# Half of a weight loaded beside the attention, the prompt's operand sums spread over the steps, and a load count in the last product

## The chip, the cores and the metric

The kernel runs on one NeuronCore of one Trainium2 chip. The metric is the device time of one execution in microseconds. The engines have names of their own in the profile: PE (TensorE, the matrix multiplier), PEld (its weight loads), DVE (VectorE), ACT (ScalarE), POOL (GpSimd) and SP (SyncE, which issues nearly all DMA transfers of this kernel). A name with a q behind it (SPq) is the engine's queue.

## The reference, cut to what matters

One layer of an encoder is run for two batches with the same weights: a prompt of 512 tokens and a sample of 1024 tokens, both 1024 channels wide, all in float32.

```
h = rmsnorm(x, norm_attn_g)
z = h @ w_in                                   # q, k, v, ca, cb
a = window_attention(q, k, v, bias, sink)      # 8 heads, 2 key/value heads, |q-k| <= 128
c = ca * sigmoid(cb)
c = dwconv31(c) + b
c = silu(layernorm(c))
x = x + concat(a, c) @ w_out
h = rmsnorm(x, norm_ffn_g)
u = dwconv3(h @ w_up) + b                      # 2 * 2816 channels
x = x + (silu(u[:2816]) * u[2816:]) @ w_down
y = rmsnorm(x, norm_final_g)
```

## The kernel before, in words

**Products.** Every float32 operand of a product is cut into a high and a low part (`hi` is a cast on ACT, `lo` a subtraction on DVE or POOL), and three matmuls stand for one: hi·hi, hi·lo, lo·hi. A matmul takes a 128x128 weight tile and 512 columns. Tokens are worked in blocks of 128: blocks 0 to 3 are the prompt, 4 to 11 the sample.

**Stages.** First comes the projection with w_in (lines 503 to 590 and 871 to 880) with the prompt's attention beside it. Then the prompt's product with w_out (`prompt_out`, line 848). Then the prompt's feed-forward up-projection: 22 steps of `ffn_step` (line 973), each of two halves of 24 matmuls; beside it runs the sample's attention, which is a generator that is advanced a piece at a time. After it come the sample's product with w_out, block by block (`out_blocks`, line 1156; each block has two halves of 512 columns, 24 matmuls a half), the sample's up-projection in a fast form with seven products a step (`first` to `seventh`, loop at line 1611, 22 steps j), and last the down-projection of both batches, again with seven products of 11 steps each (`down_step`, line 1573; the seventh product stands in a loop of its own from line 1666, with the final normalisation between its steps).

**What runs beside.** The queue `side` holds generators. `tick` (line 267) is called some times in each product and advances `side` by `pace["rate"]` pieces a call; `drain(side)` runs it to its end. `sample` (line 990) is the generator that matters here. It yields the sample's attention; then waits until the feed-forward is at its step 21 (`KW`); then loads w_out (16 pieces of 256 KB, `load_wo`, line 789) and cuts each into hi and lo (`split_wo`, line 799), first and second half of the columns in turn, five pieces behind the loads; then runs `conv_norm` (line 713: four transposes, layer norm, four transposes, the swish and the cut into hi and lo) for blocks 4 and 5. Those blocks' product needs for its first four chunks (kc 0 to 3) the attention's result, fetched back from DRAM by `load_cat` (line 708), and for its last four (kc 4 to 7) what `conv_norm` leaves. Behind the feed-forward stands `drain(side)` at line 1018, and only then the sample's blocks in order: both halves of block 4, both of block 5, and so on (line 1162).

**Sums of the prompt.** The down-projection's fast form needs sums and differences of pairs of the prompt's gated columns. `sums_of` (line 961) fetches a pair by two DMAs, makes four results on POOL (lines 966 to 969, 128x256 each) and stores them by two DMAs. In the loop over j it is called whole, at every second step from j = 2, and once more at j = 18; 11 pairs in all.

**Loads of the down-projection.** `ahead` is the list of its 185 loads in order of need; `load_next(n)` issues the next n of them, if there are any left (line 1391). `down_step` asks for three a step while fewer than 24 are held; the last loop asks for two (line 1667); `operands` asks for what is still missing.

**What sets the order.** Storage in SBUF is cut into slots (`Slots`, line 65): 15 of 4096 bytes a partition (`q`), 4 of 4352 (`c`), 61 of 2048 (`h`), 2 of 2304 (`d`). A tile takes the smallest free slot that it fits, the one that has been free longest first, and waits for whatever last read that slot. A planner (`schedule_with_timeline_sim=True`) orders the instructions of each engine by a simulated timeline, from the order in which the program issues them and what each waits for. Within `by_hand` (from line 1304) PE's order is the order written, and in the down-projection SP's too; DVE, ACT and POOL are ordered by the planner throughout.

Of the kernel before, what the change touches and what calls it, by code (L numbers as in the profile page):

```python
# [50 lines left out]
SCB, SCD = "aapa", "aaap"  # L51


WOP, WOA, DW, DW2 = 1, 5, 2, 2
NE = 2
YN = 2
OB = "cbu"
NW = 16
BL = 9
SA = 4  # L60
AP = 1
KW = 21


class Slots:
# [35 lines left out]
def tile_hybrid_encoder(ctx: ExitStack, tc: tile.TileContext, xs, rel_bias, norm_attn_g, w_in,  # L101
# [687 lines left out]
    def load_wo(kc, n):  # L789
        raw = wor[kc, n] = sb.tile([NT])  # L790
        nc.sync.dma_start(raw[:], laid["w_out"][n, :, kc, :])
# [98 lines left out]
    while out:  # L890
        if side:
            for _ in range(AP):
                if side:
                    advance(side)
            if not side:
                pace.update(late=CLO)
        advance(out)
        n += 1
        if n > 7:
            next(doubling, None)  # L900
        if n % SA == 0 and n > 18:
            next(units_of_sample)
    drain(convs)

# [56 lines left out]
    def sums_of(p):  # L961
        e, t, x, y = (sb.tile([2, HT]) for _ in range(4))
        nc.sync.dma_start(e[:], gap[1, 8][:, p])
        nc.sync.dma_start(t[:], gap[2, 4][:, p])
        eng = nc.gpsimd
        eng.tensor_tensor(x[:, 1, :], e[:, 1, :], t[:, 1, :], op=ALU.add)
        eng.tensor_tensor(x[:, 0, :], e[:, 0, :], e[:, 1, :], op=ALU.subtract)
        eng.tensor_tensor(y[:, 0, :], x[:, 1, :], e[:, 0, :], op=ALU.subtract)
        eng.tensor_tensor(y[:, 1, :], t[:, 0, :], y[:, 0, :], op=ALU.subtract)
        nc.sync.dma_start(gap[7, 5][:, p], x[:])  # L970
        nc.sync.dma_start(gap[6, 3][:, p], y[:])

    def ffn_step(k):
# [13 lines left out]
    want_up_raw(1, 0)  # L987
    at = [0]

    def sample():  # L990
        yield from units_of_sample
        while at[0] < KW:
            yield 0.0
        kt.clear(), vt.clear(), qt.clear(), bias.clear()
        use.update(norm="a")
        pace.update(rate=RN)
        for m in range(16 + WOA):
            if m in (10, 12):
                load_cat(m // 2 - 1)
            if m < 16:  # L1000
                load_wo(m // 2, m % 2)
            if m >= WOA:
                split_wo((m - WOA) // 2, m % 2, m % 4 < DW2)
                yield 0.0
        drain(late)
        for m in range(NE):
            yield from conv_norm(4 + m)

    pace.update(rate=RD, late=CD)
    for k in range(NJ):  # L1010
# [4 lines left out]
    h2.clear()  # L1015
    use.update(out=OB, turn="u")
    pace.update(rate=RE)
    drain(side)

# [137 lines left out]
        if n == 1:  # L1159
            scaled(i)  # L1160

    for i in range(4, NB - 2):
        if i + NE < NB:
            side.appendleft(conv_norm(i + NE))
        if i == 8:
            side.append(turned(1, old_bank))
        for n in range(2):
            out_blocks(i, n)
    reserve(4)
    for j in range(2):  # L1170
        for half in range(2):
# [401 lines left out]
    def down_step(k):  # L1573
# [33 lines left out]
        if i == 4 and p == 8:  # L1607
            with_x("o12", 0, 1)
            load_x1(1, 0)

    for j in range(2, NJ):
        for half in range(2):
            load_up(j + 3, half)
        if j >= NJ - 3:
            sb.free.extend(raws.free)
            raws.free.clear()
        if j >= NJ - 2:
            load_next(4)
        split_up(j + 1, 1, 2)
        if (j - 2) // 2 < NPAIR and j % 2 == 0:  # L1620
            sums_of((j - 2) // 2)
        if j == NJ - 4:
            sums_of(NPAIR - 1)
        second(j)
        sums_up(j + 1)
        sixth(j)
        split_up(j + 1, 5)
        last = j == NJ - 1
        value_part(j - 1)
        if last:  # L1630
            fourth(j, None, True)
            third(j)
        first(j + 1)
        split_up(j + 1, 6)
        seventh(j, None, not last)
        if last:
            by_hand.__exit__(None, None, None)
            by_hand = tc.manual_schedule(engines={mybir.EngineType.SP, mybir.EngineType.PE})
            by_hand.__enter__()
            load_next(10)  # L1640
            down_step(0)
        fifth(j + 1)
        split_up(j + 1, 7)
        if last:
            y_sum(j)
        else:
            fourth(j)
        gate_part(j)
        split_up(j + 1, 4)
        if not last:  # L1650
            third(j)
        split_up(j + 1, 3)
# [11 lines left out]
    z = wide()  # L1664
    OTHER = {1: 2, 3: 3, 4: 8, 6: 9, 8: 10, 9: 11}
    for p in range(NPAIR):
        load_next(2)
        make(base + p + 4)
        for tt in (0, 1):
            mm_down(z[:, tt * NT:(tt + 1) * NT], 3, p, tt)  # L1670
        if p == HOLD:
            zp = wide()
        if p >= HOLD:
            for q in range(p + 1) if p == HOLD else (p,):
                for tt in (4, 5):
                    mm_down(zp[:, (tt - 4) * NT:(tt - 3) * NT], 3, q, tt)
                hp.pop((3, q))
        if p == 4:
            for tt in (2, 3):
                zs.append(wide())  # L1680
                armed(zs[-1][:, L], hl[3, p][0][0])
                nc.scalar.copy(zs[-1][:, L], cut(o12, tt))
        if p in OTHER:
            blk = OTHER[p]
            tt = blk + 2 if blk < 4 else blk - 8
            finish(blk, (cut(u, tt), cut(e, tt)), False)
# [81 lines left out]
```

## Time and profile before

| | |
|---|---|
| median of 3 runs | 1514.33 us (1513.03, 1514.33, 1521.08) |
| the profiled execution | 1514.8 us, of which the span from its first to its last instruction is 1513.0 us |
| PE busy | 1480.5 us (98% of the span) |
| DVE, ACT, POOL busy | 1106.2, 801.7, 785.1 us |
| mean granted clock of TensorE | 0.992 |
| moved by DMA | 228.19 MB, 151 GB/s over the span |

The profile is of one execution. Busy time is the union of an engine's instructions; matmuls are pipelined and their ends are modelled, so that one of 0.39 us starts some 0.23 us after the one before it. "PEclk" is the clock that was granted to TensorE, 1.00 being full. A line such as "PE b L771 <- POOL h L803: 2.2, 1, 2.2" in the table of waits says: PE, before an instruction of line 771 that writes a tile named b, waited for an instruction of line 803 on POOL that writes a tile named h; 2.2 us in total, once, 2.2 us the longest. Line 1032 is the helper `sub`, 1029 the helper `add`, 1036 the helper `split_of`, 154 and 155 the helper `split`, 143 `load_x`, 148 `chunk_raw`.

### The profile page before, as it was taken

What the parts mean: (1) busy time and instruction counts of PE and PEld (TensorE: products, weight loads), DVE (VectorE), ACT (ScalarE), POOL (GpSimd) and SP (SyncE); (2) the same over time, 40 slices, a digit from 0 to 9 for tenths busy, and PEclk for the clock granted to TensorE, in tenths of its full rate; (3) what the DMA queues carried; (4) which work ended last, traced back from release to release, by engine and by line L of the source; (5) the groups of instructions that cost most, each with busy time, mean ns of one, the idle gap of its engine ahead of it and who ended that gap; (6) DMA issues with size and microseconds to landing.
All of it is one profiled execution on the core that took longest, in us unless ns stands there. A gap on an engine that the chain in (4) does not pass through costs nothing. (4 is left out here: it accounts for less than half of the span.)

```text
span 1513.0 us, 19880 instructions
## 1 busy us (share of the span) xinstructions
PE 1480.5 (98%) x6736; PEld 1216.5 (80%) x6736; DVE 1106.2 (73%) x1508; ACT 801.7 (53%) x1421; POOL 785.1 (52%) x691
## 2 busy tenths in 40 slices
PE   8999999999999999999999999999999999999997
PEld 7888788877888888778788788888888888888876
DVE  7877945648999895665767888888776855657865
ACT  6424455467777876653464445444454453443345
POOL 3454353356987875342436566565565211215666
PEclk9999999999999999999999999999999999999998
DMA  9455241843443444763124333333343473446744
GB/s 372 168 162 150 85 108 36 252 145 126 147 129 129 132 139 136 260 203 99 70 73 151 132 133 126 127 126 130 129 151 123 164 272 102 133 151 213 236 155 162
DMA packets 125201, 228.19 MB, mean 151 GB/s; under 512 B 20483, under 2 KB 45827, under 8 KB 124972
## 3 DMA queue, kind: packets, MB, share of 16 engines
q1 hardware_dynamic: 123564, 225.32, 45.4%
q10 hardware_dynamic: 1536, 1.61, 0.3%
q8 instruction: 53, 0.87, 0.2%
q14 instruction: 48, 0.39, 0.1%
HBM read 166.83 MB, written 61.10 MB: 151 GB/s over the span
## 5 line engine op out<-in xcount | busy, mean ns | idle before, releaser
L155 POOL TENSOR_TENSOR q<-q,q 128x1024 fp32r<-128x1024 f32 x66 | 158.6, 2406 | 76.2 <-ACT q L154 58.4
L1032 DVE TENSOR_TENSOR h<-h,h 128x512 fp32r<-128x512 f32 (+1 forms) x155 | 134.3, 891 | 82.9 <-ACT h L1036 36.4
L1032 POOL TENSOR_TENSOR q<-q,q 128x512 fp32r<-128x512 f32 x81 | 117.1, 1455 | 116.4 <-ACT q L1134 116.4
L1477 PE MATMUL w<-h,h 128*128 128x512 f32 x444 | 173.7, 391 | 1.3 <-ACT h L1460 0.8
L1479 PE MATMUL w<-h,h 128*128 128x512 f32 x436 | 170.1, 390 | 0.0
L1478 PE MATMUL w<-h,h 128*128 128x512 f32 x428 | 167.4, 391 | 2.8 <-DVE h L1032 2.8
L289 PE MATMUL u<-h,q 128*128 128x512 f32 x384 | 151.2, 395 | 0.3 <-DVE h L251 0.3
L291 PE MATMUL u<-h,q 128*128 128x512 f32 x384 | 150.4, 392 | 0.0
L290 PE MATMUL u<-h,q 128*128 128x512 f32 x384 | 150.2, 392 | 0.0
L1148 PE MATMUL w<-h,q 128*128 128x512 f32 x368 | 143.9, 391 | 2.9 <-ACT w L1237 2.6
L1150 PE MATMUL w<-h,q 128*128 128x512 f32 x368 | 143.7, 391 | 0.0
L1149 PE MATMUL w<-h,q 128*128 128x512 f32 x347 | 135.5, 390 | 0.0
L1032 POOL TENSOR_TENSOR h<-h,h 128x512 fp32r<-128x512 f32 (+1 forms) x36 | 48.5, 1348 | 161.9 <-ACT h L1460 109.6
L1036 ACT CAST h<-h 128x512 fp32r<-128x512 f32 x119 | 71.4, 620 | 109.3 <-DVE h L1032 43.6
L1477 PEld LDWEIGHTS w<-h,h 128*128 128x128 f32 x444 | 83.8, 189 | 19.7 <-ACT h L1460 1.2
L154 ACT CAST q<-q 128x1024 fp32r<-128x1024 f32 x66 | 69.1, 1049 | 54.5 <-PE u L290 31.1
L326 DVE SCALAR_TENSOR_TENSOR c<-d,cvw,c 128x512 f32<-128x512 f32 x128 | 95.9, 749 | 1.6
L1478 PEld LDWEIGHTS w<-h,h 128*128 128x128 f32 x428 | 80.7, 189 | 20.0 <-DVE h L1032 3.4
L1479 PEld LDWEIGHTS w<-h,h 128*128 128x128 f32 x436 | 82.1, 188 | 17.1
L1032 POOL TENSOR_TENSOR c<-q,c 128x512 fp32r<-128x512 f32 x46 | 72.5, 1586 | 41.8 <-ACT c L1134 41.8
L318 POOL TENSOR_TENSOR h<-h,h 128x512 f32<-128x512 f32 x62 | 80.5, 1300 | 17.9 <-ACT h L317 15.7
L1148 PEld LDWEIGHTS w<-h,q 128*128 128x128 f32 x368 | 69.1, 188 | 18.6 <-ACT w L1237 3.0
(455 smaller groups left out, 4010.9 us busy)
## 6 DMA issues: line engine op xcount, KB each, us to landing
q<-in_laid_w_up SPq DMA_DIRECT2D x88, 512.0 KB, 3.8
ga<-q SPq DMA_DIRECT2D x65, 256.0 KB, 2.2
h<-gap SPq DMA_DIRECT2D x57, 256.0 KB, 3.5
h<-ga SPq DMA_DIRECT2D x57, 256.0 KB, 3.2
h<-in_w_down SPq DMA_DIRECT2D x52, 256.0 KB, 3.3
q<-in_laid_w_in SPq DMA_DIRECT2D x22, 512.0 KB, 3.9
gap<-h SPq DMA_DIRECT2D x44, 256.0 KB, 2.8
q<-in_x_sample SPq DMA_DIRECT2D x15, 512.0 KB, 7.1
```

What stands on the lines that cost most here:

```text
L155: (nc.vector if dve else nc.gpsimd).tensor_tensor(lo[:], raw[:], hi[:].bitcast(F32), op=ALU.subtract)
L289: nc.tensor.matmul(out, whi[:, kc, :], hi[:], start=(kc == 0), stop=False)
L290: nc.tensor.matmul(out, whi[:, kc, :], lo[:], start=False, stop=False)
L291: nc.tensor.matmul(out, wlo[:, kc, :], hi[:], start=False, stop=(kc == KC - 1))
L326: nc.vector.scalar_tensor_tensor(acc[:], src(t), w(t), acc[:], op0=ALU.mult, op1=ALU.add)
L1032: (eng or nc.vector).tensor_tensor(out, a, b, op=ALU.subtract)
L1148: nc.tensor.matmul(out, whi[:, s], hi[:], start=(start and c == 0), stop=False, **go)
L1149: nc.tensor.matmul(out, whi[:, s], lo[:], start=False, stop=False, **go)
L1150: nc.tensor.matmul(out, wlo[:, s], hi[:], start=False, stop=(stop and c == 3), **go)
L1477: nc.tensor.matmul(out, sh[:, c], th[:], start=(p == 0 and not seeded), stop=False, **go)
L1478: nc.tensor.matmul(out, sh[:, c], tl[:], start=False, stop=False, **go)
L1479: nc.tensor.matmul(out, sl[:, c], th[:], start=False, stop=(p == NPAIR - 1), **go)
```

## The change

- `sample` no longer waits for step 21. From step 16 (`KL`) on, while the attention still runs, the first half of w_out's columns is loaded, in four pairs of 512 KB; a pair takes a slot of 4096 bytes or more.
- When the attention has ended, block 4's attention result is loaded, then the second half of w_out a piece at a time, each beside the cut of a piece of the first half; then `conv_norm(4)`; then the cuts of the second half, with block 5's load at their third; then, behind the last of them (`WN`), `conv_norm(5)`. Three of four cuts have their subtraction on DVE and one on POOL (`DW2` 3; half and half before).
- The `drain(side)` behind the feed-forward goes. The sample's blocks start with (4, first half), (5, first half), (4, second half), (5, second half), and before each the side queue is advanced until that block's `conv_norm` and the last piece of that half of w_out are there.
- `sums_of` becomes a generator with four stops, advanced three times a step of j from j = 2; what may be left is made at the start of the last step. Its first store is issued right behind the second result.
- `load_next(2)` in the last product's loop becomes `load_next(LN)` with `LN` = 3.
- In the loop over `prompt_out` a second period `SA2` is used from n = 99 on; it is 4, as `SA` is.

```diff
-WOP, WOA, DW, DW2 = 1, 5, 2, 2
+WOP, WOA, DW, DW2 = 1, 5, 2, 3
-SA = 4
+SA, N2, SA2 = 4, 99, 4
+KL, WN = 16, 7
+LN = 3
-KW = 21
...
+        yield
         eng = nc.gpsimd
         eng.tensor_tensor(x[:, 1, :], e[:, 1, :], t[:, 1, :], op=ALU.add)
+        yield
         eng.tensor_tensor(x[:, 0, :], e[:, 0, :], e[:, 1, :], op=ALU.subtract)
+        nc.sync.dma_start(gap[7, 5][:, p], x[:])
+        yield
         eng.tensor_tensor(y[:, 0, :], x[:, 1, :], e[:, 0, :], op=ALU.subtract)
+        yield
         eng.tensor_tensor(y[:, 1, :], t[:, 0, :], y[:, 0, :], op=ALU.subtract)
-        nc.sync.dma_start(gap[7, 5][:, p], x[:])
         nc.sync.dma_start(gap[6, 3][:, p], y[:])
...
+    fit = set()
+
+    def fitted(i):
+        yield from conv_norm(i)
+        fit.add(i)
+
     def sample():
-        yield from units_of_sample
-        while at[0] < KW:
+        for _ in units_of_sample:
             yield 0.0
+            if at[0] >= KL and not wor:
+                for kc in range(0, KC, 2):
+                    load_wo_pair(kc, 0)
         kt.clear(), vt.clear(), qt.clear(), bias.clear()
...
-        for m in range(16 + WOA):
-            if m in (10, 12):
-                load_cat(m // 2 - 1)
-            if m < 16:
-                load_wo(m // 2, m % 2)
-            if m >= WOA:
-                split_wo((m - WOA) // 2, m % 2, m % 4 < DW2)
-                yield 0.0
+        load_cat(4)
+        for kc in range(KC):
+            load_wo(kc, 1)
+            split_wo(kc, 0, kc % 4 < DW2)
+            yield 0.0
         drain(late)
-        for m in range(NE):
-            yield from conv_norm(4 + m)
+        yield from fitted(4)
+        for kc in range(KC):
+            if kc == 2:
+                load_cat(5)
+            split_wo(kc, 1, kc % 4 < DW2)
+            yield 0.0
+            if kc == WN:
+                yield from fitted(5)
...
-    drain(side)
...
-    for i in range(4, NB - 2):
-        if i + NE < NB:
-            side.appendleft(conv_norm(i + NE))
-        if i == 8:
+    turns_out = [(4, 0), (5, 0), (4, 1), (5, 1)] + [(i, n) for i in range(6, NB - 2) for n in range(2)]
+    for i, n in turns_out:
+        if n == 0:
+            (side.append if i < 8 else side.appendleft)(fitted(i + NE))
+        if (i, n) == (8, 0):
             side.append(turned(1, old_bank))
-        for n in range(2):
-            out_blocks(i, n)
+        while not (i in fit and (KC - 1, n) in wo):
+            advance(side)
+        out_blocks(i, n)
...
+    prompt_sums = chain(*(sums_of(p) for p in range(NPAIR)))
     for j in range(2, NJ):
...
+        if j == NJ - 1:
+            for _ in prompt_sums:
+                pass
...
-        if (j - 2) // 2 < NPAIR and j % 2 == 0:
-            sums_of((j - 2) // 2)
-        if j == NJ - 4:
-            sums_of(NPAIR - 1)
+        next(prompt_sums, None)
         second(j)
         sums_up(j + 1)
+        next(prompt_sums, None)
         sixth(j)
...
         first(j + 1)
         split_up(j + 1, 6)
+        next(prompt_sums, None)
         seventh(j, None, not last)
...
-        load_next(2)
+        load_next(LN)
```

More of the change, by code (lines that the diff above doesn't have):

```diff
@@ L900, in tile_hybrid_encoder @@
             next(doubling, None)
-        if n % SA == 0 and n > 18:
+        if n > 18 and n % (SA if n < N2 else SA2) == 0:
             next(units_of_sample)
```

## The prediction

> **What bounds the kernel now.** I read the page's busy shares first, then busy time by stage, then PE's waits, and last the instructions around the longest of those waits.
>
> ```profile
> PE 1480.5 (98%) x6736; PEld 1216.5 (80%) x6736; DVE 1106.2 (73%) x1508; ACT 801.7 (53%) x1421; POOL 785.1 (52%) x691
> ...
> 560.00:630.00 70.00, 70.00 (x340) 58.49 (x339) 42.18 (x85) 41.78 (x84) 33.86 (x29) 1.00 0.52 159
> 630.00:665.00 35.00, 31.42 (x142) 24.35 (x141) 23.27 (x33) 20.47 (x40) 17.87 (x17) 0.95 0.72 254
> 665.00:744.00 79.00, 79.00 (x387) 65.42 (x386) 47.89 (x75) 33.08 (x67) 25.03 (x33) 1.00 0.37 117
> ...
> 830.00:850.00 20.00, 17.41 (x77) 13.93 (x76) 15.13 (x14) 7.22 (x10) 8.08 (x7) 1.00 0.31 110
> 850.00:1190.00 340.00, 339.65 (x1481) 277.77 (x1480) 276.34 (x249) 171.75 (x255) 208.54 (x156) 1.00 0.42 138
> ...
> 1455.00:1485.00 30.00, 24.85 (x100) 19.28 (x99) 24.08 (x20) 16.61 (x39) 20.20 (x22) 0.89 0.13 49
> ```
>
> The columns of a stretch are its length, then busy us (and instructions) of PE, PEld, DVE, ACT and POOL, then PE's clock, the DMA share and GB/s. PE is the bound nearly everywhere. The change adds no matmul and takes none away, so it can only move what PE loses: its idle time, and matmuls at a lower clock. Of the stages that the diff touches, the attention beside the feed-forward (560 to 630) and the long sample loop (850 to 1190) lose nothing or 0.35 us. Three short places lose: the change from feed-forward to the sample's w_out (630 to 665: 35 - 31.42 = 3.6 us idle, clock 0.95), one early step of the sample loop (2.6 us) and the start of the last product (5.15 us, clock 0.89).
>
> ```profile
> PE w L1478 <- DVE h L1032: 2.8, 1, 2.8
> PE w L1148 <- ACT w L1237: 2.6, 1, 2.6
> ...
> PE b L771 <- POOL h L803: 2.2, 1, 2.2
> PE w L1479 <- POOL d L1032: 1.6, 1, 1.6
> ...
> PE u L770 <- DMA h<-catd: 0.9, 1, 0.9
> ```
>
> The third and fifth rows are the first place, the second row is the second, the first and fourth are the third place (with 0.8 us more).
>
> **Part 1: w_out's first half earlier, and the blocks in halves.** Before, all 16 loads stand behind the attention, so they land when the feed-forward is over, and the cuts follow them:
>
> ```profile
> 635.84 1.75 SPq L791 DMA_DIRECT2D h<-in_laid_w_out  x4
> ...
> 643.98 0.90 SPq L791 DMA_DIRECT2D h<-in_laid_w_out  x2
> ```
> ```profile
> 653.75 0.80 PE L771 MATMUL b<-h,h 128*128 128x512 f32 x1 [2.25 <-POOL h L803]
> ...
> 657.18 0.39 PE L771 MATMUL u<-h,h 128*128 128x512 f32 x1
> 657.41 0.40 PE L772 MATMUL u<-h,h 128*128 128x512 f32 x1
> ```
>
> PE waits 2.25 us for a cut on POOL, and its next eight matmuls take 657.18 - 653.75 = 3.43 us, where eight at the later spacing (657.41 - 657.18 = 0.23) would take 1.8: 1.6 us lost at half pace. With the 0.9 us for the attention's result the place costs 0.9 + 2.25 + 1.6 = 4.75, and 0.3 us of small gaps: 5.1 us.
>
> The Trainium skill ("TensorE: Matmul & The Clock Gate", section "What's actually happening") has the array drop to half clock only after at least one idle window of about 3.4 us. By that rule the 2.25 us wait would not bring half pace, and taking it away would give the wait alone, 3.5 us for the place. The trace shows the half pace right behind that wait, so the 1.6 us stay in the sum.
>
> After the change block 4's first half needs the eight cuts of the first half only, and their raw data came during steps 16 to 21 of the feed-forward. What the cuts cost:
>
> ```profile
> L803 DVE TENSOR_TENSOR h<-h,h x20: 658/692/1775, 280.2 to 657.2; 128x512 fp32r<-128x512 f32 x20
> L803 POOL TENSOR_TENSOR h<-h,h x8: 1262/1294/1772, 637.6 to 656.6; 128x512 fp32r<-128x512 f32 x8
> ```
>
> All eight POOL cuts lie at this place. With three of four on DVE, four remain: POOL loses 4 x 1.29 = 5.2 us, DVE gains 4 x 0.69 = 2.8 us, and both have room (17.9 and 23.3 busy of 35). ACT's 16 casts stay. The cuts of the second half fall beside the 48 matmuls of (4, first) and (5, first), 48 x 0.23 = 11 us. SP issues 12 transfers for 16; the four pairs go past its w_up loads, onto DMA engines that are 0.52 busy in that stretch, with some 2.1 MB over about 70 us, 30 GB/s more. I cost that at nothing, with that cover; without it, it is the third rival.
>
> What is late next is `conv_norm(4)`, which block 4 needs from its fifth chunk on. It ran from PE's transposes to DVE's last subtraction, 641.1 to 657.2, with cuts standing in its way on ACT:
>
> ```profile
> 641.14 0.66 PE L729 MATMUL a<-ident,h 128*128 128x128 f32 x4
> ```
> ```profile
> 648.27 1.51 ACT L750 ACTIVATE h<-a,vecs 128x128 f32<-128x128 f32 x4 [0.69 <-PE a L744]
> 649.66 1.67 ACT L802 CAST h<-h 128x512 fp32r<-128x512 f32 x3
> 651.21 0.64 ACT L751 ACTIVATE h<-h 128x512 f32<-128x512 f32 x1
> ```
> ```profile
> 655.58 1.66 DVE L754 TENSOR_TENSOR h<-h,h 128x512 fp32r<-128x512 f32 x1
> ```
>
> Now the second half's cuts are issued behind it; I estimate its end 4 to 6 us earlier, near 652 (1.7 us on ACT above, some 1 us on DVE's stretched subtraction, the rest in DVE and POOL cuts). PE's cover until then is the first four chunks of four half blocks, 4 x 12 x 0.23 = 11 us from 639.7 on, up to about 651. So the long wait goes, the half pace with it, and about 1 us stays. I take 3.8 of the 5.1 us; bounds 0 (the chain becomes the wait) and 5.1.
>
> **Part 2: the prompt's sums in pieces.** The 2.6 us wait comes down a chain: POOL was without a gap from 816 to 833, with one pair's four results within (3.5 us), DVE waited for it, ACT for DVE, PE for ACT.
>
> ```profile
> 817.55 0.74 POOL L967 TENSOR_TENSOR h<-h 128x256 f32<-128x256 f32 x1
> ...
> 821.22 0.74 POOL L966 TENSOR_TENSOR h<-h,h 128x256 f32<-128x256 f32 x1
> 822.04 0.74 POOL L968 TENSOR_TENSOR h<-h,h 128x256 f32<-128x256 f32 x1
> ...
> 824.44 1.28 POOL L969 TENSOR_TENSOR h<-h,h 128x256 f32<-128x256 f32 x1
> ...
> 829.17 2.54 POOL L1032 TENSOR_TENSOR q<-q,q 128x512 fp32r<-128x512 f32 x2
> ```
> ```profile
> 831.72 1.79 DVE L1032 TENSOR_TENSOR h<-q 128x512 f32<-128x512 f32 x1 [3.72 <-POOL q L1032]
> 833.44 1.21 DVE L1285 TENSOR_TENSOR q<-q,c 128x1024 f32<-128x1024 f32 x1
> ```
> ```profile
> 834.68 0.62 ACT L1134 CAST c<-q 128x512 fp32r<-128x512 f32 x1 [5.49 <-DVE q L1285]
> 835.21 0.58 ACT L1237 COPY w<-w 128x512 f32<-128x512 f32 x1
> ```
>
> The program issued those four at step 4; the planner drew them into step 3. Cut up, 44 results and 44 DMAs stay as many: four stops a pair and three advances a step put two or three results into each step from the second to about the 17th, instead of four at every other. In this step that takes one or two from POOL, 0.7 to 2 us. The wait is 2.6 us, so it may shrink to nothing, or hardly. A gain of 1.3 us is the middle; bounds 0 and 2.6. Elsewhere PE hides the sums (339.65 of 340 us busy). Behind the moved DMAs on SP stand w_up loads that are asked for three steps ahead, which costs nothing. A pair's four 2048-byte tiles are now held all the time; that too falls under PE's full stretch.
>
> **Part 3: three loads a step.** Counting `load_next` through: 4 + 4 + 10 loads ahead of the first step, 8 at it, then three a step while fewer than 24 are held. The 185th goes out in the last step of the sixth product. The last product finds the list empty, and its load count is without effect. The trace agrees: SP's last such load, and the first of the two additions that read out the sixth product, are
>
> ```profile
> 1451.12 0.33 SPq L1416 DMA_DIRECT2D h<-in_w_down  x1
> ```
> ```profile
> 1456.00 1.21 DVE L1029 TENSOR_TENSOR q<-w,q 128x1024 f32<-128x1024 f32 x1
> ```
>
> So the 5.15 us of the third place are not touched: there DVE's cuts stand in its queue behind the normalisation (POOL's and ACT's results), not behind a transfer. Nothing, with bounds in the second rival. `SA2` equals `SA`: nothing.
>
> **The sum.** 1514.8 us (span 1513.0 and 1.8 around it) - 3.8 - 1.3 = 1509.7 for a profiled execution. That execution lies 0.5 us above the median of the runs shown, 1514.33, so I predict **1509.3** as median; its own range, from the bounds of both parts, is 1506.6 to 1514.3.
>
> **The rivals.**
>
> 1. *The wait only changes its owner.* `conv_norm` takes the place of the cuts: chain and cover above end within about 1 us of each other (652 and 651), and `conv_norm(5)` is now issued behind all cuts. For it: that near tie. Against: four fewer cuts on POOL. Only part 2 counts: 1514.3 - 1.3 = 1513.0.
>
> 2. *The last product gains as well.* Its waits come from the order that the planner gave DVE, ACT and POOL, and that order may shift with the slots that the earlier parts leave. For it: 2.8 + 1.6 + 0.8 us of waits, then seven matmuls from 1479.58 to 1482.73, 3.15 us for 1.6, as the rows below show; 6.7 us together. Against: no edit is aimed there, and a shift may go the other way, by as much. Then 1509.3 - 6.7 = 1502.6.
>
> ```profile
> 1479.58 0.79 PE L1478 MATMUL w<-h,h 128*128 128x512 f32 x1 [2.77 <-DVE h L1032]
> ...
> 1482.73 0.52 PE L1479 MATMUL w<-h,d 128*128 128x512 f32 x1
> ```
>
> 3. *The pairs take the slots of the w_up loads: slower.* Four slots of 4096 bytes or more are held from step 16 to the cuts, and w_up's raw chunks and their cuts live in the same slots. These loads already wait for PE to free one, up to 6.6 us:
>
> ```profile
> SPq L148 <- PE u L291: 12.7, 5, 6.6
> ```
> ```profile
> 612.81 2.41 POOL L155 TENSOR_TENSOR q<-q,q 128x1024 fp32r<-128x1024 f32 x1 [1.93 <-ACT q L154]
> ```
> ```profile
> 631.09 0.78 ACT L939 ACTIVATE h<-u,vecs,fw 128x512 f32<-128x512 f32 x1 [0.25 <-PE u L291]
> ```
>
> The last chunk is cut by 615.2 and used when the half step before it ends, about 631: 15.8 us in hand. A chunk that gets its slot a whole step later (two halves of 7 us) and waits 6.6 us again comes 20.5 us late, and PE stands for 4.7 us. From the second such half on (9.4 us, 1.6 at half pace) all gain is gone: 1509.3 + 11 = 1520.3; with three 1525. Against: four `c` slots are free by then, the convolutions being over.
>
> **How the numbers follow.** About 0.5% (7.6 us) is what a measurement of this kernel can tell from no change: faster is below 1506.8, slower above 1521.9. Forecast 0.42 (0.06 of it below 1506.8, where small gaps go too), first rival 0.25, second 0.23 (all below), third 0.10 (0.06 of it above 1521.9). Faster 0.29, slower 0.06, same 0.65. For 8 in 10 the range runs from 1502, which leaves out the lower part of the second rival, about 0.09, to 1517.5, which leaves out most of the third, about 0.09.
>
> **What would show it.** Step 1 right: no wait of PE above 1 us between the feed-forward's last matmul and the first block's end, a clock of 1.00 there, w_out loads of 512 KB ahead of the feed-forward's end; wrong: a wait for line 753 or 754 there. Step 2 right: the wait for line 1237 under 1.5 us, four prompt sums never back to back. Step 3 right: no load of the list behind the first matmul of the last product. The prediction is wrong if PE waits within the last five feed-forward steps, or if the last product's waits change by more than 3 us either way.

## The result, and the profile after

| | before | after |
|---|---|---|
| median, side by side, 10 runs each | 1517.26 us (1513.03 to 1521.08) | 1524.99 us (1519.97 to 1526.28) |
| ratio after to before | | 1.0050, 95% interval 1.0034 to 1.0065 |
| the profiled execution | 1514.80 us (span 1513.0) | 1525.28 us (span 1523.5) |
| feed-forward's end and sample's w_out: last feed-forward matmul to first matmul of the sample loop | 107.4 us | 103.95 us |
| sample loop: its first matmul to the first of the down-projection | 433.5 us | 445.3 us |

The change made the kernel slower, by 0.5%. All of that, and more, arises in the sample loop. The marks that separate the stages are these rows of PE's timeline (start, duration, instruction), of before and then of after; the code after has moved down by 15 to 17 lines (line 1148 is now 1163, 1477 is 1494, 1264 is 1281, `sub` is 1047, `add` is 1044).

```profile
744.68 0.40 PE L1148 MATMUL w<-h,q 128*128 128x512 f32 x1
...
1178.20 0.39 PE L1477 MATMUL w<-h,h 128*128 128x512 f32 x1
```
```profile
741.89 0.40 PE L1163 MATMUL w<-h,q 128*128 128x512 f32 x1
...
1187.17 0.39 PE L1494 MATMUL w<-h,h 128*128 128x512 f32 x1
```

The loop starts 2.8 us earlier and the down-projection 9.0 us later, so the loop takes 11.8 us more; from there to the end 1.5 us are added (the last matmuls start at 1506.7 and 1517.2, and the output follows). -2.8 + 11.8 + 1.5 = 10.5 us, the difference of the two profiled executions.

The page's busy times and the stages after, with the columns as in the prediction:

```profile
PE 1482.7 (97%) x6736; PEld 1216.0 (80%) x6736; DVE 1113.2 (73%) x1512; ACT 802.2 (53%) x1421; POOL 786.1 (52%) x687
```
```profile
560.00:630.00 70.00, 70.00 (x340) 58.55 (x339) 42.30 (x85) 43.10 (x83) 36.66 (x30) 1.00 0.49 154
630.00:665.00 35.00, 32.91 (x157) 26.09 (x156) 23.98 (x39) 20.73 (x41) 11.09 (x14) 1.00 0.71 236
...
850.00:1199.00 349.00, 341.61 (x1483) 277.63 (x1482) 277.83 (x250) 171.14 (x255) 213.02 (x156) 1.00 0.40 135
1464.00:1495.00 31.00, 24.54 (x98) 18.85 (x96) 25.07 (x21) 17.39 (x41) 21.36 (x21) 0.94 0.18 68
```

No engine has more work: the work of the long loop is the same, 1481 and 1483 matmuls, 249 and 250 instructions on DVE, 156 on POOL. But PE, which had stood for 0.35 us of 340, now stands for 7.4 of 349. Over the whole loop the idle times of PE's rows add up to 4.2 us before and 12.3 after. These 8.1 us are most of the 11.8; the other 3.7 lie in matmuls that follow each other more slowly and in gaps too short to be listed. 1.6 of them are eight matmuls from 824.99 on, 0.42 us apart, where the granted clock was 0.50 (825.0 to 828.4). PE's table of waits says what it stands for:

```profile
PE w L1163 <- ACT c L1281: 8.5, 5, 2.5
PE w L1495 <- DVE h L1047: 3.0, 1, 3.0
...
PE w L1496 <- POOL d L1047: 1.6, 1, 1.6
```

The second and third row are the last product's waits, as before (2.8 and 1.6). The first is new: five waits of PE for ACT's depthwise operation, every second or fourth step. The wait that part 2 aimed at, for the copy of line 1237, is gone. Followed back, one of the five looks so; the rows are of all engines' timelines, in order of time, and the bracket is the idle time before and what ended it:

```profile
974.20 0.67 DVE L1047 TENSOR_TENSOR h<-q,q 128x512 f32<-128x512 f32 x1
974.90 0.32 SPq L1317 DMA_DIRECT2D ga<-h  x1
977.98 0.72 DVE L1047 TENSOR_TENSOR h<-q 128x512 f32<-128x512 f32 x1 [3.11 <-DMA ga<-h]
...
983.83 0.69 DVE L1044 TENSOR_TENSOR w<-w,h 128x512 f32<-128x512 f32 x1
984.55 1.21 ACT L1281 ACTIVATE c<-w,vecs,fw 128x1024 f32<-128x1024 f32 x1 [5.53 <-DVE w L1044]
985.84 0.47 PE L1163 MATMUL w<-h,c 128*128 128x512 f32 x1 [1.94 <-ACT c L1281]
...
996.49 1.29 POOL L1047 TENSOR_TENSOR q<-h,q 128x512 fp32r<-128x512 f32 x1
```

DVE makes the last operand of an odd step (`y` in `value_part`), SP stores it at 974.90, and DVE's next instruction is the sum for the third product (the first `sub` of `sums_up`). It writes a 2048-byte tile, and has been given the slot that `y` has just left: it stands 3.11 us until the store has read that slot. DVE works in order, so the addition of line 1044 behind it comes late, ACT's depthwise operation after it, and PE, which needs the bank that ACT reads, stands 1.94 us.

Why that slot can be counted from the program: `Slots` hands out the slot that has been free longest. Before, the third sum finds 8 free slots of 2048 bytes and takes one that was left 20 to 27 tile allocations earlier (at steps 4 to 18). With a pair's four tiles held all the time it finds 4, and at steps 4, 8, 12, 16 and 18 it takes `y`'s, left 14 allocations earlier (by step 18 eight are free again). At steps 7, 11 and 15 it takes one that a pair of the prompt left five allocations earlier; there DVE stands 0.9 to 1.0 us for POOL's line 973.

The tile names of the built program show one thing more: the planner puts each of the five sums that get `y`'s slot behind the sum of the step after it. The sum at 977.98 is that of step 12 and comes behind that of step 13. It is made 18.5 us ahead of its cut into hi and lo (the last row), and the other four 17 to 21 us. In the kernel before, the sums of steps 5 to 18 are made 34 to 45 us ahead.

### The profile page after: what moved, and what is told of

It is laid out like the page before. It is cut to its first block, busy times and chain, and to the rows that moved or that the text cites. A ratio compares the mean times of both kernels' runs of the same rounds, so it can differ in the third digit from the quotient of the medians.

```text
span 1523.5 us, 19867 instructions
## 1 busy us (share of the span) xinstructions
PE 1482.7 (97%) x6736; PEld 1216.0 (80%) x6736; DVE 1113.2 (73%) x1512; ACT 802.2 (53%) x1421; POOL 786.1 (52%) x687
## 5 line engine op out<-in xcount | busy, mean ns | idle before, releaser
L1047 POOL TENSOR_TENSOR q<-q,q 128x512 fp32r<-128x512 f32 x81 | 123.6, 1538 | 112.1 <-ACT q L1149 107.2
L292 PEld LDWEIGHTS u<-h,q 128*128 128x128 f32 x384 | 72.1, 188 | 14.8
```

What stands on the lines that cost most here:

```text
L292: nc.tensor.matmul(out, wlo[:, kc, :], hi[:], start=False, stop=(kc == KC - 1))
L1047: (eng or nc.vector).tensor_tensor(out, a, b, op=ALU.subtract)
```

## The experiments

Times are compared with the kernel before on the same chip. "Loop" is the length of the sample loop in the profiled execution, measured between the same two marks; "stands" is the sum of DVE's idle times right before the third sums, from 790 to 1180 us, whatever ended them: not all of it is a wait for a slot.

| kernel | ratio to before, 95% interval | loop, us | DVE stands, us |
|---|---|---|---|
| before | 1 | 433.5 | 9.6 |
| after | 1.0050 (1.0034 to 1.0065) | 445.3 | 19.1 |
| 1 w_out part alone | 0.9986 (0.9974 to 0.9998) | 432.6 | 8.3 |
| 2 spread sums alone | 1.0060 (1.0045 to 1.0075) | 445.3 | 19.6 |
| 3 before, third sum takes `y`'s slot | 1.0033 (1.0020 to 1.0045) | 438.9 | 11.8 |
| 4 after, third sum never takes it | 1.0044 (1.0028 to 1.0060) | 442.7 | 17.7 |
| 5 w_out part, whole sums in two tiles | 0.9998 (0.9988 to 1.0008) | 436.9 | 4.4 |
| 6 the same, four slots withheld | 1.0096 (1.0083 to 1.0109) | 452.2 | 33.1 |
| 7 after, sums in two tiles | 0.9985 (0.9977 to 0.9994) | 434.8 | 5.0 |
| 8 the same, `y`'s slot never taken | 1.0059 (1.0045 to 1.0072) | 448.0 | 18.0 |
| 9 after, one slot kept for the third sum | 1.0047 (1.0034 to 1.0061) | 442.8 | 39.6 |
| 10 as 7, one slot kept | 1.0122 (1.0103 to 1.0140) | 455.3 | 48.2 |
| 11 as 1, cuts half and half | 0.9999 (0.9989 to 1.0009) | 433.2 | 8.2 |
| 12 as 5, two slots kept, in turn | 1.0028 (1.0014 to 1.0042) | 440.8 | 9.5 |
| 13 as 7, two slots kept | 1.0089 (1.0071 to 1.0107) | 450.4 | 10.0 |
| 14 as 1, two slots kept | 1.0055 (1.0039 to 1.0071) | 443.0 | 19.1 |
| 15 as 5, two slots withheld | 1.0014 (1.0001 to 1.0027) | 435.8 | 11.3 |

### 1 and 2: each part alone

Kernel 1 is the change without its edits of `sums_of`, of the calls to it, and with `LN = 2`. Kernel 2 is the kernel before with only these edits of the sums:

```diff
+    prompt_sums = chain(*(sums_of(p) for p in range(NPAIR)))
     for j in range(2, NJ):
...
-        if (j - 2) // 2 < NPAIR and j % 2 == 0:
-            sums_of((j - 2) // 2)
-        if j == NJ - 4:
-            sums_of(NPAIR - 1)
+        next(prompt_sums, None)
         second(j)
         sums_up(j + 1)
+        next(prompt_sums, None)
```

> The kernel before with the w_out part alone (pairs, order of the half blocks, cuts three to one); the prompt's sums whole as before, two loads a step. Slot theory (the loss comes from the sums holding four 2048-byte slots, so that the third sum of w_up is written to the slot whose store to DRAM is still running) and POOL theory (the loss comes from the sums' results standing between the cuts on POOL): the gain of the w_out place alone, 2 to 4 us off, ratio 0.997 to 0.999, no wait for line 1264's activation in the sample loop. Early-part theory (the loss comes from the slots that the w_out part leaves): the loop loses about 10 us here too, ratio 1.004 or more.

> The kernel before with the spread sums alone. Slot theory and POOL theory: the loop from the first of its matmuls to the first of the down-projection takes some 10 to 12 us more, ratio 1.006 to 1.009; by the slot theory with PE's longest waits every fourth step, where the third sum takes the slot of the odd step's last operand. Early-part theory: no loss, ratio 0.998 to 1.001.

The parts add up: 0.9986 and 1.0060 make 1.0046, and the change had 1.0050. PE's waits of kernel 2 in the sample loop are those of after, and those of kernel 1 are those of before:

```profile
PE w L1152 <- ACT c L1268: 6.9, 5, 2.0
PE w L1154 <- POOL q L1036: 1.5, 2, 1.0
```
```profile
PE w L1159 <- ACT w L1250: 2.0, 1, 2.0
```

So the spread sums cost some 9 us (0.0060 x 1517), and the w_out part gains 2.1 us (0.3 to 3.9).

### 3 and 4: the one slot

In kernel 3 the kernel before is made to give the third sum `y`'s slot at those five steps; in kernel 4 the kernel after is made never to give it:

```diff
+            if j in (4, 8, 12, 16, 18) and last_y[0] in sb.free:
+                sb.free.remove(last_y[0])
+                sb.free.insert(0, last_y[0])
             t = third_sum[j] = sb.tile([NT])
```
```diff
+            if last_y and last_y[0] in sb.free:
+                sb.free.remove(last_y[0])
+                sb.free.append(last_y[0])
             t = third_sum[j] = sb.tile([NT])
```

> The kernel before, sums whole, with one thing changed: at j = 4, 8, 12, 16 and 18 the third sum of w_up is given the slot that the last operand of the odd step before has just left (its store to DRAM may be running). Slot theory: VectorE waits for that store, and PE five times for 1 to 2.5 us, 6 to 11 us in all, ratio 1.004 to 1.007. POOL theory and early-part theory: no change, ratio 0.999 to 1.001.

> The changed kernel with one thing changed: the third sum of w_up never takes the slot that the last operand has just left; that slot goes to the end of the list of free ones. Slot theory: the waits for the store go, the loop is back within 3 us of the kernel before, and with the w_out part's gain the kernel is level with the one before or up to 4 us faster, ratio 0.997 to 1.001. POOL theory and early-part theory: as the changed kernel, ratio 1.004 to 1.006.

Half of the theory stands. The slot alone, with no sum spread, brings the stall on `y`'s store and costs 0.33%. That is less than was expected of it, and PE's waits are others: 3.0 us in five for line 1223 and 2.0 us in three for line 1241, none over 1.4 us. In kernel 4, without that slot, the loss stays, for the third sum now gets a slot that the stores of the spread sums still read. DVE's waits in the sample loop, of kernel 4:

```profile
DVE h L1047 <- DMA gap<-h: 10.6, 5, 4.7
```

With four slots free, the one handed out has been left 5 to 21 tile allocations earlier, against 20 to 27 in the kernel before. The one slot is thus not the whole cause; two readings are left, how many slots are free, and how long ago they were left (their age).

### 5 to 8 and 15: as many slots, and spreading without the shortage

In kernels 5, 7 and 8 the four results of a pair are written over operands that are no longer needed, so that a pair holds two tiles; 5 makes them whole, 7 and 8 spread them. (In all of them the results also go to DRAM in other pairs.) Kernels 6 and 15 are kernel 5 with four and two slots kept out of use:

```diff
-        e, t, x, y = (sb.tile([2, HT]) for _ in range(4))
+        e, t = sb.tile([2, HT]), sb.tile([2, HT])
...
-        eng.tensor_tensor(x[:, 0, :], e[:, 0, :], e[:, 1, :], op=ALU.subtract)
+        eng.tensor_tensor(e[:, 1, :], e[:, 0, :], e[:, 1, :], op=ALU.subtract)
```
```diff
+        if j == 2:
+            withheld = [s for s in sb.free if s[0][0] == "h"][:4]
+            for s in withheld:
+                sb.free.remove(s)
+        if j == 17:
+            sb.free.extend(withheld)
```

> The w_out part alone, with the prompt's sums made whole as before the change, but in two tiles of 2048 bytes instead of four (each result written over an operand that is no longer needed). The third product's sum then finds 8 free slots, as with whole sums in four tiles. Shortage theory (the loss comes from the number of free 2048-byte slots while the sample loop runs: 8 before, 4 after the change): no loss, 0.997 to 1.000 of the time before, as the w_out part alone had (0.9986); no wait of PE for line 1281's copy, none of DVE's sum for a store. Pace theory (the loss comes from POOL's results being spread over the steps, whatever slots they hold): the same, 0.997 to 1.000, since nothing is spread. It is the control of the next kernel.

> As the control with whole sums in two tiles, but four 2048-byte slots are kept out of use from step 2 to step 17 of the sample loop: the third product's sum finds 4 free, as after the change, and takes the slot that the odd step's last operand left one step before at every even step from 4 to 18, eight times where the changed kernel does it five times. No sum is spread. Shortage theory: the loss of the change is there without the change's edit, 1.004 to 1.010 of the time before, with DVE's sum waiting about 3 us for the store and PE waiting for ACT's depthwise operations, eight times rather than five. Pace theory: no loss, 0.997 to 1.001.

> The changed kernel, sums spread as it spreads them, but made in two tiles instead of four: two 2048-byte slots are held at a time, the third product's sum finds 6 free, and takes the just-left slot of the last operand three times (steps 6, 10, 14), one to two tile allocations later than in the changed kernel. Shortage theory: part of the loss goes, 0.999 to 1.004 of the time before, three waits or fewer of PE in the sample loop. Pace theory: the loss stays, 1.004 to 1.007, five waits.

> As the spread sums in two tiles, and the third product's sum never takes the slot that the last operand has just left (it goes to the end of the list); with 6 free slots it takes slots that were left 13 to 22 tile allocations ago. Shortage theory: nearly all of the loss goes, 0.996 to 1.001 of the time before, no wait of PE over 1.5 us in the sample loop's even steps, no wait of DVE's sum for a store. Pace theory: the loss stays, 1.004 to 1.007.

> As the control with whole sums in two tiles, with two 2048-byte slots kept out of use from step 2 to step 17 instead of four. The third product's sum finds 6 free slots, left 20 and 25 tile allocations ago (14 and 11 with four withheld). If the loss follows how recently the slots were left: none, 0.998 to 1.001 of the time before, a sample loop of 433 to 437 us. If it follows the number of free slots: about half of the loss of four withheld, 1.003 to 1.006, a loop of 442 to 446 us.

Kernel 6 shows that fewer free slots are enough: four slots withheld cost 0.98% against kernel 5, more than the change did, without any spreading. Part of that size has no counterpart in the change. PE stands 6.63 us right after the slots were taken away, because a copy on ACT waits for a store of the prompt's sums:

```profile
811.40 0.59 ACT L1241 COPY h<-w 128x512 f32<-128x512 f32 x1 [4.80 <-DMA gap<-h]
...
812.03 0.80 PE L1159 MATMUL w<-h,q 128*128 128x512 f32 x1 [6.63 <-ACT h L1241]
```

Kernel 7 shows that the edit of the change, with two tiles held instead of four, costs nothing. It does not test the pace of POOL's results, for the planner put the four results of each pair together again. In all eleven pairs of kernel 7 the last of the four starts 2.4 to 6.1 us after the first; here is one pair:

```profile
1052.58 0.74 POOL L968 TENSOR_TENSOR h<-h,h 128x256 f32<-128x256 f32 x1
1053.39 0.74 POOL L970 TENSOR_TENSOR h<-h 128x256 f32<-128x256 f32 x1
1054.21 0.74 POOL L972 TENSOR_TENSOR h<-h,h 128x256 f32<-128x256 f32 x1
1055.03 0.74 POOL L975 TENSOR_TENSOR h<-h,h 128x256 f32<-128x256 f32 x1
```

In the changed kernel only three pairs are really drawn apart (16 to 17 us); the other eight take 3.3 to 7.4 us, as nearly all pairs do in the kernel before (3.3 to 7 us, the last one 11.5). So no run spreads the results on POOL without a shortage, and the pace theory is left without a test of its own. Against it speaks that kernel 6 loses as much without any spreading. DVE's waits before the third sum in kernel 6 and in kernel 7 (the rows of the view that stand before these sums, over 1 us):

```profile
DVE h L1043 <- POOL q L1043: 13.4, 7, 2.0
DVE h L1043 <- DMA ga<-h: 6.7, 4, 2.2
DVE h L1043 <- issue: 6.1, 3, 2.5
DVE h L1043 <- DMA gap<-h: 4.0, 1, 4.0
DVE h L1043 <- POOL c L1043: 2.7, 1, 2.7
```
```profile
DVE h L1047 <- issue: 3.0, 2, 1.6
DVE h L1047 <- DMA ga<-h: 1.5, 1, 1.5
```

Kernel 15 tells number from age. Two slots withheld take the free ones from 8 to 6, but leave the third sum with slots nearly as old as in kernel 1 (20 and 25 allocations against 20 and 27). The loop stays at 435.8 us, as the age reading has it. The ratio, 1.0014 (1.0001 to 1.0027), lies between the two forecasts, nearer to that of age (up to 1.001) than to that of number (from 1.003). Kernel 8 missed: it has as many free slots as kernel 7 and only hands them out in another order (13 to 22 allocations old, 16 to 25 in kernel 7), and yet loses 0.74% against it. Its slots are older than those of the changed kernel (5 to 21), and its loop is longer. Most of DVE's idle time before the third sums (11.3 of 18.0 us) ends there with a load of w_up, which is the sum's own operand, and not with a reader of its slot:

```profile
DVE h L1047 <- DMA q<-in_laid_w_up: 11.3, 5, 4.8
```

### 9, 10 and 12 to 14: slots of its own for the third sum

```diff
+        if j == 2:
+            own.append(sb.tile([NT]))
+        if j == NJ - 4:
+            own.clear()
...
-            t = third_sum[j] = sb.tile([NT])
+            t = third_sum[j] = own[0] if own else sb.tile([NT])
```

In 12 to 14 there are two such tiles, used in turn.

> The changed kernel, with one edit: from step 2 to step 18 of the sample loop the third product's sum is written to a 2048-byte slot that is kept for it alone, so it waits for nothing but the two cuts that read the sum of the step before. The sums stay spread and in four tiles; the other results of the step share the slots that are left, and ACT's copies now take slots that the stores of the sums have just left (5 tile allocations ago, at every other step). Theory of the third sum's slot (VectorE, working in order, stands before the third sum until a transfer has read its slot, and what is queued behind it comes late to ACT and to PE): the loss of the sample loop goes, 0.997 to 1.001 of the time before, VectorE's waits before the third sum under 6 us in all (about 20 us in the changed kernel, 10 us before). Theory of the shortage in general (any of the step's results that gets a just-left slot costs as much): half of the loss or more stays, 1.002 to 1.007, with PE waiting for ACT's copies. Pace theory: 1.004 to 1.007.

> The spread sums in two tiles, and one slot kept for the third product's sum as in the kernel with its own slot. Theory of the third sum's slot: no wait of VectorE before the third sum over 1 us, and a time at or a little below that of the spread sums in two tiles: 0.996 to 0.999 of the time before. Theory of the shortage in general: the same or a little worse, 0.998 to 1.002, since ACT's copy of the sixth product now takes the last operand's slot one step after it was left, at every odd step.

> The w_out part with whole sums in two tiles, and two slots kept for the third product's sum from step 2 to step 20, used in turn: the slot was last read by the cuts of two steps before. No other result of a step gets a slot left less than 10 tile allocations ago. If VectorE's stall before the third sum carries the loss: no wait of VectorE before the third sum over 0.5 us, the sample loop 431 to 434 us long (433.5 before the change), 0.996 to 0.999 of the time before. If the stall is only a companion of the loss: a loop as long as without the two slots (436.9 us), 0.999 to 1.001.

> Spread sums in two tiles, and two slots kept for the third product's sum, used in turn. ACT's copy of the fifth product now takes the last operand's just-left slot at steps 5, 9 and 13 (6 tile allocations old). If the stall before the third sum carries the loss: no such wait over 0.5 us and a loop of 432 to 436 us, 0.997 to 1.000 of the time before. If any just-left slot costs as much: 439 us or more, 1.001 to 1.005, with PE waiting for ACT's copy of the fifth product.

> The w_out part with the prompt's sums whole and in four tiles, as before the change, and two slots kept for the third product's sum. If the stall before the third sum carries what is left of waits in the sample loop: no such wait over 0.5 us beside the one behind POOL's four sums at step 3, a loop of 431 to 433 us (432.6 with the w_out part alone), 0.996 to 0.999. If the stall is a companion: no change against the w_out part alone, 0.998 to 1.000.

None brought the loop back. Kernel 9 has the time that the shortage in general gives, though with DVE standing rather than ACT's copies; the other four are slower than any theory said, and than the same kernels without the kept slots (7, 5, 7 and 1). Kernel 10, the slowest of all, shows why, in DVE's waits in the sample loop and in a piece of POOL's and DVE's timelines:

```profile
DVE h L1047 <- POOL q L1047: 46.5, 14, 7.5
```
```profile
942.02 1.29 POOL L1047 TENSOR_TENSOR q<-h,q 128x512 fp32r<-128x512 f32 x1
...
943.35 1.21 DVE L1047 TENSOR_TENSOR h<-q 128x512 f32<-128x512 f32 x1 [7.51 <-POOL q L1047]
```

The sum is cut into hi and lo for the seventh product, and POOL's cut (the only one that reads an `h` tile) comes last. With one slot the next sum can't be made until then: it starts 0.04 us after the cut has ended, 7.51 us after DVE was ready for it. In the kernel before DVE runs further ahead. The two sums of these rows are cut 34 and 45 us later, since the cuts of one and of two earlier sums come first (from step 5 on sums and cuts go in the same order here, one a step of 19.5 us):

```profile
901.39 0.98 DVE L1032 TENSOR_TENSOR h<-q 128x512 f32<-128x512 f32 x1
907.51 0.68 DVE L1032 TENSOR_TENSOR h<-q 128x512 f32<-128x512 f32 x1
...
935.54 1.29 POOL L1032 TENSOR_TENSOR q<-h,q 128x512 fp32r<-128x512 f32 x1
...
952.26 1.28 POOL L1032 TENSOR_TENSOR q<-h,q 128x512 fp32r<-128x512 f32 x1
```

So up to three sums are alive at once, and the planner makes them in pairs. One slot allows one, 17 to 24 us ahead (kernels 9 and 10; kernel 6, with four slots withheld, has the same distance from step 4 on, 18 to 24 us), and two slots allow two, evenly spaced. A kept slot takes freedom away, too. Kernels 12 and 13 show as well that the stall before the sum is not the whole loss: DVE stands there no longer than before the change (9.5 and 10.0 against 9.6 us), yet the loops are 7.3 and 16.8 us longer than before. In kernel 13 PE waits for POOL's cuts instead:

```profile
PE w L1166 <- POOL q L1047: 8.1, 3, 2.8
```

### 11: the cuts of w_out

```diff
-WOP, WOA, DW, DW2 = 1, 5, 2, 3
+WOP, WOA, DW, DW2 = 1, 5, 2, 2
```

> The w_out part alone, but with the cuts of w_out half on VectorE and half on POOL as before the change, instead of three to one. If the early loads and the order of the half blocks carry the gain, the time is that of the w_out part alone, 0.998 to 1.000 of the time before. If the three-to-one cuts carry it, PE waits for a POOL cut again, 1 to 2 us at the start of the sample's product, and the time is 0.999 to 1.001.

The gain of kernel 1 is gone (0.9999), though the intervals of the two overlap. PE waits again at the start of the sample's product, not for a cut on POOL but for a cast on ACT and a result of DVE:

```profile
641.62 0.66 PE L730 MATMUL a<-ident,h 128*128 128x128 f32 x4 [1.61 <-DVE h L670]
...
649.93 1.22 PE L771 MATMUL u<-h,h 128*128 128x512 f32 x2 [2.08 <-ACT h L803]
```

From the last feed-forward matmul to the first of the sample loop it takes 108.5 us, against 104.8 in kernel 1. By these figures the early loads alone bring nothing here, and with three of four cuts on DVE they do; the overlap leaves that open.

## Why the prediction was wrong

**The step that failed** is in part 2: "A pair's four 2048-byte tiles are now held all the time; that too falls under PE's full stretch." The trace had shown PE busy for 339.65 of 340 us, and I read that as cover. As I read it now, it was a balance that needs the other engines to be ahead, and being ahead needs slots: a result can be made early only into a slot that has been read already. The change took four of eight free slots for nearly the whole of the stretch. I had looked at what the sums cost in instructions (nothing: as many, as long) and at the queue of SP, and not at what their tiles displaced. I gave the step bounds of 0 and 2.6 us of gain; it cost 11.8 us in the profiled loop, and 0.60% of the time, some 9 us, where it was made alone (kernel 2). Of the 15.7 us between the forecast, 1509.3, and the measured 1524.99, 7.7 are the loss of the change, 5.0 the gain that was forecast, and 2.9 the start: the forecast counted from a median of three runs, 1514.33, and side by side the kernel before had 1517.26.

**What part 2 aimed at** came in part. The 2.6 us wait for line 1237 is gone. But the results were not put in ones and twos into the steps: the planner kept most pairs together, and four sums stand back to back once, which the prediction had named as a sign against this step:

```profile
790.23 1.78 POOL L968 TENSOR_TENSOR h<-h,h 128x256 f32<-128x256 f32 x1
791.96 0.75 POOL L970 TENSOR_TENSOR h<-h 128x256 f32<-128x256 f32 x1
792.67 0.74 POOL L973 TENSOR_TENSOR h<-h,h 128x256 f32<-128x256 f32 x1
793.49 0.75 POOL L975 TENSOR_TENSOR h<-h,h 128x256 f32<-128x256 f32 x1
```

What the edit is worth without the shortage, kernel 7 says. Against the kernel before its loop gains nothing: the one wait of 2.6 us becomes four of 2.9 us together, and the loop is 434.8 us long, against 433.5. Against its control, kernel 5, with the same two tiles and the sums whole, the loop is 2.1 us shorter and the ratio 0.9985 instead of 0.9998, with intervals that overlap. A gain of the size forecast, 1.3 us, is neither shown nor excluded.

**Part 1** was right in kind. No wait of PE falls between 560 and 630 us, the loads of 512 KB go out ahead of the feed-forward's end, and `conv_norm` did not take the place of the cuts; the slots of the w_up loads were not missed (third rival). PE's waits at the place after, over 0.5 us:

```profile
642.22 0.50 PE L772 MATMUL c<-h,h 128*128 128x512 f32 x1 [0.70 <-DVE h L804]
643.52 0.63 PE L730 MATMUL a<-ident,h 128*128 128x128 f32 x4 [0.57 <-issue]
644.73 0.50 PE L681 MATMUL a<-h,h 128*128 128x512 f32 x1 [0.58 <-DVE h L691]
```
```profile
557.10 0.81 SPq L796 DMA_DIRECT2D q<-in_laid_w_out  x2
```

The size was uncertain: 3.8 us forecast, 2.1 (0.3 to 3.9) measured. The terms of the 5.1 us were one execution's. Kernels 2 and 3 run the same code at this place as the kernel before, and in their profiled executions the wait for POOL's cut was 1.2 us, with no half pace behind it: here kernel 2, whose next eight matmuls take 1.95 us.

```profile
654.67 0.50 PE L771 MATMUL b<-h,h 128*128 128x512 f32 x1 [1.20 <-POOL h L803]
...
656.62 0.39 PE L771 MATMUL u<-h,h 128*128 128x512 f32 x1
```

The stage takes 105.4 us there, not 107.4, and 103.5 to 104.8 in kernels 1, 5 and 7 and after. For that execution two of the terms, 2.25 and 1.6 us, are thus too large by 2.65 us, while the waits for the attention's result are larger than forecast, 1.8 us instead of 0.9. The half pace is no fixed price of such a wait: it followed one of 2.25 us in the kernel before and one of 2.53 us after (at 824.99, the next matmuls 0.42 us apart), not the one of 2.6 us in the kernel before. In the execution of kernel 1 it stood at this very place, from 646.36 to 650.1, behind waits of only 0.70, 0.57 and 0.58 us. The Trainium skill ("TensorE: Matmul & The Clock Gate", section "What's actually happening") asks for an idle window of some 3.4 us, and calls the effect variable from run to run, since the window runs freely. The variation agrees with these runs; the length does not, as none of the idle times just named reached 3.4 us.

**Part 3** was right: with `LN` = 2 the program has the same instructions in the same order on every engine. The list's last load goes out at 1461.90, ahead of the last product, whose waits are of the size they had (6.5 us against 5.2).

**The rivals.** None of them held what happened. Rival 3 was the only slower one and gave nearly the right time, 1520.3 to 1525, but by another mechanism at another place, with slots of 4096 bytes in the feed-forward. The kind of danger was the right one; I looked for it where the diff holds large tiles longer, not where it holds small ones.

**What is settled, and what is not.** Shown: the loss comes from the edit of the sums (2); the same edit with two tiles held instead of four does not bring it (7); and withholding four slots brings a loss without that edit (6). Shown too: other ways of handing out the slots cost time with as many or nearly as many free (3, 8, 10, 12 to 14), and a smaller number with old slots costs little (15). Not tested alone: the pace of POOL's results, as kernel 7 does not spread them there. Not settled: which stall carries the loss. DVE's before the third sum goes with it in most kernels but not in 9, 12 and 13. How far ahead the sums are made does not decide it alone either: in the changed kernel five of them are made only 17 to 21 us ahead, but in kernel 7 three (steps 6, 10 and 14, 20 to 21 us) at hardly any cost, and in kernel 8 none of steps 4 to 20 comes under 27 us, and its loop is 13 us longer than that of kernel 7. The planner orders DVE, ACT and POOL by the slots too, so that each other order of slots is also another order of instructions, as the swapped sums show; a kernel that changes the slots and keeps the order wasn't tried. Kernel 8 is explained by neither count nor age alone.

**The better version.** Kernel 1 (the w_out part alone) and kernel 7 (the whole change, sums in two tiles) are both faster than both kernels: 0.9986 and 0.9985 of the time before, 2.1 us (0.3 to 3.9) and 2.3 us (0.9 to 3.5).

## What to carry to other kernels

Count free buffers as a resource with a price: when an edit holds tiles longer, list what else takes tiles of that size in the stage, how many stay free, and who last reads the slot that each would get, stores included. An engine at 100% in a stage is not cover in itself: its feeders must be able to run ahead of it, and buffers bound how far they can. Look, too, at what the planner made of an edit before taking its run as a test: here sums that the program spread came out of it in fours. A buffer kept for one user alone is no cure where that user comes back before its last reader is done: here a rotation over all free ones let three results be alive, a kept one only one.

## What the runs showed that was not expected

Taking four of eight free 2048-byte slots away cost 15 us in a loop of 437 us (kernels 5 and 6; 6.6 of them in one wait), while every engine but PE was busy for less than 83% of it. A store's read of its source tile held an in-order engine for 3.1 us, from 974.87 to 977.98; the store was issued 0.03 us after the tile had been written. And the same instructions at the same place cost 5.1 us in one execution and 3.3 and 3.5 in two others (1.14 + 0.66 + 0.28 + 1.20 in kernel 2), so a single profile's small waits are samples, not prices.
